# Recurrent gates from unsplit fp32 blocks, recurrence as timed events, modulation from fp32 quarter products, later sums of squares

## The chip, the cores and the metric

One core of one Trainium2 chip runs the whole program. The metric is device time in microseconds; an execution is one forward pass. The program is fixed before it starts: every engine (PE for matrix products, DVE, ACT and POOL for elementwise work, SP for issuing transfers) has its own queue, which it works off in order.

## The reference

Two layers (DEPTH = 2) over 1024 latent tokens and 256 context tokens of width 1024:

```python
m = silu(cond) @ w_mod + b_mod                  # shift, scale, gate; for c and for c_ctx
h = rmsnorm(x, norm_g) * (1 + scale) + shift
q, k, v, ga, u, gb, gm = split(h @ w_in)
# A: attention, 16 query heads, 4 key heads, q and k RMS-normalised per head of 64, rotary
# B: recurrence, for each of two directions d, on uc = centred_conv(u):
r = sigmoid(block_diag(uc, w_gates[d][0]) + b)  # 16 diagonal blocks of 64 x 64
i = sigmoid(block_diag(uc, w_gates[d][1]) + b)
log_a = -8 * r * softplus(-lam[d]); a = exp(log_a)
h_t = a_t * h_(t-1) + sqrt(1 - a_t**2) * (i * uc)_t      # direction 1 runs backwards
y = h_dir0 + h_dir1
x = x + gate * ((sigmoid(gma) * (o * silu(ga)) @ w_a + sigmoid(gmb) * (y * silu(gb)) @ w_b) @ w_out)
```

The context runs through the same weights; the last layer leaves out its context outputs.

## The kernel before

Features lie on the 128 partitions, tokens along the free axis, in three chunks: C (256 context tokens), L0 and L1 (512 latent tokens each). Every large product is a `gemm` of 8 contraction steps with three matmuls each (weights and input are both split into a rounded part and a remainder: hi·hi, hi·lo, lo·hi), in the type fp32r. `w_load` fetches a 1024 x 128 weight tile in two halves, `w_split` splits it one tile ahead: the rounded part on the engine named by `weng` ("a" is ACT, "g" is POOL), the remainder on DVE.

PE's order is written out by hand. A `Timeline` keeps an estimate of PE time (`mm` adds each matmul's cost), `tl.at(delay, fn)` puts an event on a heap, and `tl.fill(gen)` steps a generator of matmuls and runs each event that has come due. The orders of ACT, DVE, POOL and SP are made by the tile scheduler from the same program. PSUM has six buffers of the tag "s" (also "g") and two of "av". Two rings in SBUF are shared by many users: `mix` (4 buffers of 128 x 1286) and `sm` (3 of 128 x 512).

The stages in order:

- The prologue (from L606): one transfer after another brings w_mod in eight tiles of 1 MB and x in three chunks. `modulation` (L323) multiplies the two conditioning vectors by a w_mod tile in four fp32 products with a stationary operand of 2 columns; `mod_turn` copies the 2 rows out, turns them by transposes onto the partitions, and `mod_done` adds the bias. `scale_rows` makes the sums of squares of x and scales it; `modulate` makes h. `recurrent_consts` (L195) works out constants of the recurrence for each layer on DVE.
- Queries, keys and values. `Group.evac` (L464) copies a tile out and squares it; `Group.sums`, due 4.0 later, adds the squares per head with `ssq` matmuls.
- The recurrent stage (from L774), eight tiles `Lru(t)` of 128 features. Each has a gemm for u (1280 tokens) and one for the gate path g. `conv` makes uc when u is out, then splits it (`uh`, `ul`). `gate` (L820) runs twelve times a tile, for two directions, two gates and three chunks: three fp32r matmuls with a 128 x 128 block that is zero off its two diagonal 64 x 64 blocks, then a tanh on ACT out of PSUM. `coeffs` (L836) then writes the whole rest at once: exp, tanh and square on ACT, the scaled products on DVE, square roots on ACT, one product per direction on POOL, three scans on DVE, and the merge with `g2`, which goes to DRAM as `zb`. `a`, `b`, `tr` and `ti` have one buffer per direction. `evac_g` (L870) takes the tanh of g on ACT and, 0.9 later, multiplies it on DVE by g, which is read out of PSUM.
- Attention, woven with the remaining input products; it is not touched.
- The output stage. In layer 0 `modulation_side` (L346) makes sixteen blocks of 256 columns of modulation beside the products: ACT scales each w_mod piece by each conditioning value (16 operations a block), POOL adds them up (`macc`), the sum is split (`mhi` on ACT, `mlo` on DVE), and four fp32r matmuls with the selector `cond_sel` add over the partitions; `mod_turn` follows.

Of the kernel before, what the change touches and what calls it, by code (L numbers as in the profile page):

```python
# [39 lines left out]
KT = 8  # L40
# [60 lines left out]
def trunk_kernel(ctx: ExitStack, tc: tile.TileContext, xT, cc, par, wmod, win, wgate, wo,  # L101
# [45 lines left out]
    def tr(o, a):  # L147
# [5 lines left out]
    DMA.dma_start(par_sb, par)  # L153
# [4 lines left out]
    e2 = sm("e2")  # L158
    V.memset(e2[:, 0:4], 0.0)
    V.memset(e2[:, 0:4:3], 1.0)  # L160
    cond_sel = const.tile([128, 2, 2], F32R, name="condsel")
    V.tensor_copy(cond_sel, e2[:, 0:4].rearrange("p (a b) -> p a b", a=2))
# [9 lines left out]
                    pattern=[[-1, 128]], channel_multiplier=1)  # L172

# [7 lines left out]
    cs = const.tile([128, KT, 2], F32, name="cs")  # L181
    ct = const.tile([128, KT, 2], F32, name="ct")
    S.activation(ct, cc_sb, AF.Tanh, scale=0.5)
    V.scalar_tensor_tensor(cs, ct, 1.0, cc_sb, op0=OP.add, op1=OP.mult)
    V.tensor_scalar(cs, cs, 0.5, None, op0=OP.mult)
# [7 lines left out]

    def recurrent_consts(l):
        lam = p(l, "lam", 0, 16)  # L195
        t = const.tile([128, 6, 16], F32, name="spt", tag="spt")
# [124 lines left out]
    def modulation(l, i, b, half, wm, box):  # L321

        if half == 0:  # L323
            box["ps"] = ptile("s", "modps")
        ps = box["ps"]
        for k in range(4):
            mm(ps[0:2], cs[:, 4 * half + k], wm[:, k], half == 0 and k == 0, half == 1 and k == 3)
            tl.pump()
        if half == 1:
            mod_turn(l, 4 * b, 4, ps, 1.0)  # L330

    def mod_turn(l, i, n, ps, wait):

        row = sm("mrow")
        S.activation(row[0:2, 0:n * 128], ps[0:2, 0:n * 128], AF.Copy)

        def turn():
            pt = ptile("s", "modpt")
            for j in range(n):
                tl.now += 0.109  # L340
# [5 lines left out]
    def modulation_side(l, blocks, work):  # L346

        for hb in [2 * b + i for b in blocks for i in range(2)]:
            acc = work.tile([128, 2, 256], F32, name="macc", tag="macc")
            for k in range(KT):  # L350
                if k % 4 == 0:
                    wm = mix("wm")[:, 0:1024].rearrange("p (k n) -> p k n", k=4)
                    DMA.dma_start(wm, wmod[l, k * 128:(k + 4) * 128, hb * 256:(hb + 1) * 256]
                                  .rearrange("(k p) n -> p k n", p=128))
                w = wm[:, k % 4]
                t = acc if k == 0 else sm("wmt").rearrange("p (s n) -> p s n", s=2)
# [4 lines left out]
                yield  # L361

            for _ in range(4):
                yield
            hi = sm("mhi", F32R).rearrange("p (s n) -> p s n", s=2)
            lo = sm("mlo", F32R).rearrange("p (s n) -> p s n", s=2)
            S.activation(hi, acc, AF.Copy)
            V.tensor_sub(lo, acc, r32(hi))
            for _ in range(3):
                yield  # L370
            ps = ptile("av", "modps")
            for x, part in enumerate((hi, lo)):
                for s in range(2):
                    mm(ps[0:2, 0:256], cond_sel[:, s], part[:, s], x + s == 0, x + s == 2)
            mod_turn(l, 2 * hb, 2, ps, 3.0)
# [76 lines left out]
    class Group:  # L452
# [10 lines left out]
        def evac(self, i, c, ps):  # L463
# [9 lines left out]
            if c == part[-1]:  # L473
                tl.at(4.0, lambda: self.sums(i, part, o))
# [134 lines left out]
    with tc.tile_pool(name="prep", bufs=1, reuse_waits="tile") as work:  # L609
        xs, arrive = {}, {}  # L610
# [15 lines left out]
        def scale_rows(c):  # L626
# [18 lines left out]
            def bcast():  # L645
# [4 lines left out]
                for k in range(KT):  # L650
                    if c == "L1":
# [10 lines left out]
        def modulate(c, k0, nk=4):  # L662

            n = CH[c][1]
# [676 lines left out]
```

## Time and profile before

| | us |
|---|---|
| median of 3 runs | 3177.37 (lowest 3171.86) |
| profiled execution, its own time | 3176.29 |
| profiled execution, span from first to last instruction | 3174.5 |
| PE busy in it | 3049.5 |

A row of the profile names an engine, a line of the kernel and `output<-inputs` by the program's names (L145 is the helper that issues all matmuls, so the output's name tells them apart). The length of a matmul's row goes on beyond the start of the next; what one costs in a row of many is the distance between starts.

### The profile page before, as it was taken

The page shows a single profiled execution, that of the slowest core. Times are in us where ns is not written, and L with a number is a line of the kernel's source. Part 1 is how long each engine was busy: PE and PEld are TensorE (multiplying, and loading weights), DVE is VectorE, ACT ScalarE, POOL GpSimd, SP SyncE. Part 2 cuts the span into 40 slices and gives each one's busy share as a digit, 9 for nine tenths or more (in the row PEclk, how much of TensorE's full clock was granted, in tenths as well). Part 3 has the DMA queues.
Part 4 walks back from the last instruction along what each step waited for, and adds up shares of the span by engine and source line. Part 5 has one row for each costly group of instructions (what it writes and reads, how often), then busy time and mean ns, then how long its engine had stood idle before and what let it go on. Part 6 is the DMA issues. An engine that isn't in the chain of part 4 may idle for free.

```text
span 3174.5 us, 42428 instructions
## 1 busy us (share of the span) xinstructions
PE 3049.5 (96%) x14592; PEld 2459.1 (77%) x14592; DVE 2453.9 (77%) x3675; ACT 1715.0 (54%) x3060; POOL 1024.5 (32%) x777
## 2 busy tenths in 40 slices
PE   7999999999999999999999999999999999999999
PEld 3788778788777777887777778777777777777887
DVE  7665887589989998556685776897799989996544
ACT  4323767466666666445654324676476666663222
POOL 0211444134334434245522222333244444441000
PEclk9999999999999999999999999999999999999999
DMA  5443111421222222254555452111412121115554
GB/s 197 145 149 126 44 57 50 125 63 54 76 68 82 60 62 75 97 189 158 170 196 175 135 176 71 58 47 53 123 55 76 58 75 58 55 58 173 183 173 140
DMA packets 243416, 332.08 MB, mean 105 GB/s; under 512 B 63664, under 2 KB 109552, under 8 KB 242944
## 3 DMA queue, kind: packets, MB, share of 16 engines
q1 hardware_dynamic: 243200, 329.37, 32.6%
q8 instruction: 115, 1.88, 0.2%
q14 instruction: 101, 0.83, 0.1%
HBM read 252.54 MB, written 76.58 MB: 104 GB/s over the span
## 4 chain that ended last, share of the span: by engine, by line
PE 53%; DVE 19%; issue 6%; ACT 4%; DMA 4%; POOL 3%; SPq 0%; DVEq 0%; POOLq 0%; ACTq 0%
PE gps L145 29%; PE avps L145 8%; PE s2ps L145 7%; PE s1ps L145 4%; DVE pl L1008 3%; DVE wlo L227 3%; DVE mp L979 2%; PE lps L145 2%; POOL macc L360 2%; PE gtps L145 1%; DVE ti L856 1%; PE qps L145 1%; POOL b L853 1%; DVE g L867 1%; PE vps L145 1%
## 5 line engine op out<-in xcount | busy, mean ns | idle before, releaser
L145 PE MATMUL gps<-h,whi 128*128 128x512 f32 x3328 | 1042.3, 394 | 18.3 <-DVE g L876 15.9
L145 PEld LDWEIGHTS gps<-h,whi 128*128 128x128 f32 x3328 | 613.5, 190 | 135.3 <-issue 10.7
L1008 DVE TENSOR_TENSOR pl<-pf,ph 128x512 fp32r<-128x512 f32 x656 | 627.2, 957 | 71.3 <-ACT ph L1007 67.9
L145 PE MATMUL gps<-h,wlo 128*128 128x512 f32 x1664 | 655.2, 394 | 1.4 <-DVE wlo L227 1.4
L1006 ACT ACTIVATE pf<-s2ps 128x512 f32<-128x512 f32 x656 | 392.9, 599 | 343.1 <-PE s2ps L145 171.7
L1022 POOL TENSOR_TENSOR acc<-pf 128x512 f32<-128x512 f32 x256 | 353.0, 1379 | 686.4 <-ACT pf L1006 686.2
L979 DVE TENSOR_REDUCE mp<-s1ps 128x1 f32<-128x512 f32 (+1 forms) x800 | 453.7, 584 | 59.9 <-PE s1ps L145 56.5
L1007 ACT ACTIVATE ph<-s2ps 128x512 fp32r<-128x512 f32 x656 | 390.0, 595 | 0.0
L227 DVE TENSOR_TENSOR wlo<-wraw,whi 128x512 fp32r<-128x512 f32 x392 | 330.8, 865 | 62.2 <-ACT whi L226 33.0
L226 ACT ACTIVATE whi<-wraw 128x512 fp32r<-128x512 f32 x324 | 194.6, 628 | 340.9 <-PE gps L145 269.1
L145 PEld LDWEIGHTS gps<-h,wlo 128*128 128x128 f32 x1664 | 314.3, 189 | 71.4 <-DVE wlo L227 2.2
L145 PE MATMUL s1ps<-k,qa 128*128 128x512 f32 (+1 forms) x800 | 287.3, 368 | 15.9 <-DMA qa<-q0L 10.7
L145 PEld LDWEIGHTS s1ps<-k,qa 128*128 128x128 f32 x800 | 244.5, 310 | 55.4 <-DVE mp L979 10.6
L145 PE MATMUL avps<-pl,vv 128*128 128x512 f32 x656 | 262.4, 400 | 8.0 <-DVE pl L1008 7.7
L145 PE MATMUL avps<-ph,vv 128*128 128x512 f32 x656 | 266.2, 406 | 0.0
L145 PE MATMUL s2ps<-qa,k 128*128 128x512 f32 x656 | 260.8, 398 | 4.4 <-DVE mp L979 3.4
L145 PE MATMUL s2ps<-qb,k 65*128 65x512 f32 x656 | 262.5, 400 | 0.1
L145 PE MATMUL gps<-e,whi 128*128 128x512 f32 x768 | 244.8, 399 | 0.4 <-DVE e L227 0.2
L360 POOL TENSOR_TENSOR macc<-macc,wmt 128x512 f32<-128x512 f32 x112 | 156.6, 1398 | 252.3 <-ACT wmt L358 228.0
L1024 POOL TENSOR_TENSOR acc<-acc,pf 128x512 f32<-128x512 f32 x128 | 183.1, 1430 | 79.4 <-ACT pf L1006 77.4
L145 PE MATMUL qps<-h,whi 128*128 128x512 f32 x640 | 203.6, 399 | 1.7 <-DVE h L674 0.9
L145 PE MATMUL gps<-c,whi 128*128 128x256 f32 x1024 | 197.8, 289 | 2.7 <-DVE c L222 1.9
(214 smaller groups left out, 4945.0 us busy)
## 6 DMA issues: line engine op xcount, KB each, us to landing
wraw<-in_win_dram SPq DMA_DIRECT2D x200, 256.0 KB
wraw<-in_wo_dram SPq DMA_DIRECT2D x192, 256.0 KB
wm<-in_wmod_dram SPq DMA_DIRECT2D x32, 512.0 KB
wm<-in_wmod_dram SPq DMA_DIRECT2D x8, 1024.0 KB
rb<-rq SPq DMA_DIRECT2D x64, 128.0 KB
k<-k SPq DMA_DIRECT2D x24, 320.0 KB
v<-vst SPq DMA_DIRECT2D x20, 256.0 KB
vv<-v SPq DMA_DIRECT2D x8, 640.0 KB
```

What stands on the lines that cost most here:

```text
L145: nc.tensor.matmul(o, a, b, start=start, stop=stop)
L226: S.activation(dst_hi, src, AF.Copy)
L227: (V if lo_eng == "v" else G).tensor_sub(dst_lo, src, r32(dst_hi))
L360: G.tensor_add(acc, acc, t)
L853: G.tensor_mul(a2, a2, ti)
L856: V.tensor_tensor_scan(h, a, a2, 0.0, op0=OP.mult, op1=OP.add)
L979: tl.at(0.3, lambda: V.reduce_max(self.mp[:, j, b:b + 1], ps[:, :n], axis=AX.X))
L1006: S.activation(pf, ps, AF.Exp)
L1007: S.activation(ph, ps, AF.Exp)
L1008: tl.at(1.4, lambda: V.tensor_sub(pl, pf, r32(ph)))
L1022: G.tensor_add(self.acc_tile(x), first, pf)
L1024: G.tensor_add(self.accs[x], self.accs[x], pf)
```

## The change

Six edits:

1. The gates. The 64 x 64 blocks are loaded alone (`gw`) and multiplied unsplit, in fp32: per chunk eight products of 64 rows by 64 columns, in two groups of four (one per gate), each of the four on another pair of row half and column half. Direction 1 lands with its two halves of 64 features exchanged; so its constants are loaded exchanged (`recurrent_params`), uc is copied to an exchanged `us`, and its scan's output is exchanged back into `a1`, all by transfers. `gate` runs three times a tile, 3.6 apart, with four PSUM buffers at a time. The split of uc and of the blocks goes.
2. `coeffs` becomes thirteen events over 26 units of PE time. `ti` gets a second buffer; `c0` gets a buffer of its own in place of one of `mix`.
3. `evac_g` copies g out of PSUM on ACT as well; the DVE multiplication reads SBUF and is due at 2.5.
4. In the recurrent stage weights are split with ACT, as elsewhere (`weng` is no longer switched).
5. The modulation, in the prologue and beside the output stage: the stationary operand is padded to 32 columns, four products go to four quarters of the output partitions, and a matmul with `sel4` adds the quarters while it turns them.
6. `Group.sums` is due at 7.0 in place of 4.0. `recurrent_consts` waits for its later loaded parameters.

```diff
+    def recurrent_params():
+        DMA.dma_start(par_sb[:, :, lam_c:lam_c + 8], par[:, :, lam_c:lam_c + 8])
+        for a, n in ((gate_c + 16, 16), (lam_c + 8, 8)):
+            for h in range(2):
+                DMA.dma_start(par_sb[64 * h:64 * h + 64, :, a:a + n], par[64 - 64 * h:128 - 64 * h, :, a:a + n])
...
+    def mod_half(ps, half, wm, n):
+        for k in range(4):
+            mm(ps[32 * k:32 * k + 32, :n], csp[:, 4 * half + k], wm[:, k], half == 0, half == 1, 0.215 * n / 512)
...
-                nc.tensor.transpose(pt[:, 2 * j:2 * j + 2], row[0:2, j * 128:(j + 1) * 128], ident[0:2, 0:2])
+                mm(pt[:, 2 * j:2 * j + 2], row[:, j * 128:(j + 1) * 128], sel4, True, True, 0.2)
...
-                for s in range(2):
-                    S.activation(t[:, s], w, AF.Copy, scale=cs[:, k, s:s + 1])
-                if k:
-                    G.tensor_add(acc, acc, t)
...
+            for half in range(2):
+                mod_half(ps, half, wms[half], 256)
...
-                tl.at(4.0, lambda: self.sums(i, part, o))
+                tl.at(7.0, lambda: self.sums(i, part, o))
...
-        weng[0] = "g"
...
-                    self.uh, self.ul = self.wt("uh", dt=F32R), self.wt("ul", dt=F32R)
-                    split(self.uh, self.ul, uc)
...
-                    tl.at(28.0 if last else 36.0, self.gate)
+                    self.us = self.exchange(uc, self.wt("us"))
+                    self.tg = [[self.wt(f"tr{d}"), self.wt(f"ti{d}", 2)] for d in range(2)]
+                    self.todo = ["C", "L0", "L1"]
+                    tl.at(20.0 if last else 24.0, self.gate)
+                def exchange(self, a, b):
+                    DMA.dma_start(b[0:64], a[64:128])
+                    DMA.dma_start(b[64:128], a[0:64])
+                    return b
...
-                    mm(ps[:, :n], gh[:, dg], uh[:, off:off + n], True, False)
-                    mm(ps[:, :n], gh[:, dg], ul[:, off:off + n], False, False)
-                    mm(ps[:, :n], gl[:, dg], uh[:, off:off + n], False, True)
...
+                    ps = [ptile("s", "gtps") for _ in range(4)]
+                    for gi in range(2):
+                        for h in range(2):
+                            rows = slice(64 * h, 64 * h + 64)
+                            for d in range(2):
+                                o = 64 * (h ^ d)
+                                mm(ps[2 * gi + d][o:o + 64, :n], self.gw[rows, 2 * d + gi], self.uc[rows, off:off + n],
+                                   True, True, 0.03 + 0.245 * n / 512)
...
+                    for at, fn, *d in ((0, decay, 1), (0.5, gated, 1), (2, gated, 0), (4.5, decay, 0), (5, square, 1),
+                                       (9.5, square, 0), (11, root), (14, product, 1), (17, product, 0),
+                                       (17.5, scan, 1), (21.5, scan, 0), (22, self.exchange, i1, a1), (26, merge)):
+                        tl.at(at, lambda fn=fn, d=d: fn(*d))
...
+                    S.activation(g, ps[:, :n], AF.Copy)
+                    tl.at(2.5, lambda: V.scalar_tensor_tensor(g, th[:, :n], 1.0, g, op0=OP.add, op1=OP.mult))
```

## Rows read from the trace of the kernel before

**Rows 1.** The page's first part: busy time of each engine, share, instructions.

```profile
PE 3049.5 (96%) x14592; PEld 2459.1 (77%) x14592; DVE 2453.9 (77%) x3675; ACT 1715.0 (54%) x3060; POOL 1024.5 (32%) x777
```

**Rows 2.** Windows by stage: length, PE, PEld, DVE, ACT, POOL busy, clock, DMA.

```profile
250.00:575.00 325.00, 309.98 (x1578) 263.01 (x1578) 237.79 (x205) 213.13 (x259) 123.28 (x98) 0.99 0.20 65
...
1314.00:1745.00 431.00, 408.96 (x2063) 338.76 (x2062) 271.15 (x438) 220.74 (x470) 156.96 (x113) 0.97 0.54 176
...
1909.00:2225.00 316.00, 293.87 (x1382) 243.90 (x1381) 254.38 (x181) 194.03 (x236) 108.97 (x93) 0.97 0.16 54
```

**Rows 3.** PE's waits, recurrent stage of layer 0: us, times, longest.

```profile
PE gps L145 <- DVE g L876: 8.5, 7, 2.2
PE gtps L145 <- ACT ti L829: 4.8, 3, 3.0
```

**Rows 4.** The same for layer 1.

```profile
PE gtps L145 <- DVE g L876: 11.7, 3, 5.2
PE gps L145 <- DVE g L876: 7.4, 4, 2.9
```

**Rows 5.** PE's timeline, gates in the recurrent stage: start, us, instructions.

```profile
300.28 0.28 PE L145 MATMUL gtps<-uh,gh 128*128 128x256 f32 x1
...
300.64 0.63 PE L145 MATMUL gps<-h,whi 128*128 128x512 f32 x2
...
301.34 0.40 PE L145 MATMUL gtps<-uh,gh 128*128 128x512 f32 x1
...
302.04 0.40 PE L145 MATMUL gtps<-uh,gh 128*128 128x512 f32 x1
```

**Rows 6.** PE's timeline in attention: four fp32 products to four quarters.

```profile
651.92 1.06 PE L145 MATMUL lps<-acc,ones 128*32 128x512 f32 x8
652.91 0.50 PE L145 MATMUL avps<-ph,vv 128*128 128x512 f32 x1
```

**Rows 7.** Windows of one recurrent tile, layer 0.

```profile
441.50:478.20 36.70, 35.16 (x181) 29.81 (x180) 30.93 (x25) 26.23 (x32) 17.40 (x13) 1.00 0.16 54
```

**Rows 8.** Groups of instructions: ACT's weight split and a copy out of PSUM.

```profile
L226 ACT ACTIVATE whi<-wraw 128x512 fp32r<-128x512 f32 x324 | 194.6, 628 | 340.9 <-PE gps L145 269.1 <-issue 36.4 <-PE qps L145 21.8
...
L797 ACT ACTIVATE up<-gps 128x512 f32<-128x512 f32 (+1 forms) x48 | 24.2, 525 | 88.4 <-PE gps L145 88.4
```

**Rows 9.** Recurrence of one tile, ACT's and DVE's timelines: first exponential, last merge.

```profile
412.47 1.45 ACT L844 ACTIVATE a<-tr,sp 128x1280 f32<-128x1280 f32 x1
...
444.49 2.78 DVE L867 SCALAR_TENSOR_TENSOR g<-ti,g 128x512 f32<-128x512 f32 x2 [1.18 <-POOL ti L866]
```

**Rows 10.** Windows of the prologue and its end.

```profile
18.50:51.80 33.30, 27.91 (x82) 8.61 (x81) 24.08 (x59) 16.64 (x33) 0.00 (x0) 0.85 0.76 274
51.80:77.00 25.20, 21.07 (x125) 16.83 (x124) 22.88 (x52) 15.94 (x28) 0.00 (x0) 1.00 0.07 22
```

**Rows 11.** PE's timeline in the prologue.

```profile
24.11 1.05 PE L145 MATMUL ssn<-ones,sqa 128*128 128x1 f32 x8 [1.14 <-DVE sqa L395]
...
31.37 0.41 PE L341 MATMUL modpt<-ident,mrow 2*128 2x2 f32 x4
...
47.41 4.45 PE L145 MATMUL modps<-wm,cs 128*2 128x512 f32 x10
```

**Rows 12.** PE's waits, 52 to 262 us, then 1750 to 1919 us.

```profile
PE ssq L145 <- ACT sqq L472: 6.4, 3, 3.0
...
PE ssq L145 <- ACT sqq L472: 8.6, 3, 6.5
```

**Rows 13.** PE's waits, output stage of layer 0.

```profile
PE modps L145 <- ACT mhi L367: 7.4, 4, 4.3
...
PE modps L145 <- DVE mlo L368: 3.8, 6, 1.6
```

**Rows 14.** The chain of waits, 585 to 960 us: two of its transfers.

```profile
592.19 6.61 DMA qa<-q0L
...
897.79 2.30 DMA l2L<-rq
```

More of the change, by code (lines that the diff above doesn't have):

```diff
@@ L319, in mod_done, with modulation @@
             V.tensor_scalar(gt, m[:, 16:24], 0.5, None, op0=OP.mult)
-    def modulation(l, i, b, half, wm, box):
+    def mod_half(ps, half, wm, n):
+        for k in range(4):
+            mm(ps[32 * k:32 * k + 32, :n], csp[:, 4 * half + k], wm[:, k], half == 0, half == 1, 0.215 * n / 512)
+    def modulation(l, b, half, wm, box):
         if half == 0:
             box["ps"] = ptile("s", "modps")
[L325 to L328, printed above, removed]
+        mod_half(box["ps"], half, wm, 512)
+        tl.pump()
         if half == 1:
-            mod_turn(l, 4 * b, 4, ps, 1.0)
+            mod_turn(l, 4 * b, 4, box["ps"], 1.0)
     def mod_turn(l, i, n, ps, wait):
         row = sm("mrow")
-        S.activation(row[0:2, 0:n * 128], ps[0:2, 0:n * 128], AF.Copy)
+        S.activation(row[:, 0:n * 128], ps[:, 0:n * 128], AF.Copy)
         def turn():
@@ L363, in modulation_side @@
+            wms = []
+            for half in range(2):
+                wm = mix("wm")[:, 0:1024].rearrange("p (k n) -> p k n", k=4)
+                DMA.dma_start(wm, wmod[l, half * 512:half * 512 + 512, hb * 256:(hb + 1) * 256]
+                              .rearrange("(k p) n -> p k n", p=128))
+                wms.append(wm)
+                for _ in range(3):
+                    yield
             for _ in range(4):
                 yield
-            hi = sm("mhi", F32R).rearrange("p (s n) -> p s n", s=2)
@@ L366, in modulation_side @@
[L366 to L369, printed above, removed]
-                yield
[L371 to L375, printed above, removed]
+            ps = ptile("av", "modps")
@@ L378, in trunk_kernel @@
+            for half in range(2):
+                mod_half(ps, half, wms[half], 256)
+            mod_turn(l, 2 * hb, 2, ps, 3.0)
+            for _ in range(4):
+                yield
     HS = {"L0": ("h0", "h1"), "L1": ("h2", "h3"), "C": ("c0", "c1")}
@@ L650, in bcast @@
                 for k in range(KT):
+                    scaled.add(c)
                     if c == "L1":
@@ L662, in modulate @@
         def modulate(c, k0, nk=4):
+            assert c in scaled
             n = CH[c][1]
@@ L847, in coeffs @@
[L847 to L854 removed]
+                        S.activation(b, a, AF.Square)
@@ new lines, in gated, with square, root @@
+                    def gated(d):
+                        i = co[d][2]
+                        V.scalar_tensor_tensor(i, i, 1.0, self.us if d else self.uc, op0=OP.add, op1=OP.mult)
+                    def square(d):
+                        b = co[d][1]
+                        V.scalar_tensor_tensor(b, b, 1.0, self.tg[d][0], op0=OP.add, op1=OP.mult)
+                    def root():
+                        for d in range(2):
+                            S.activation(co[d][1], co[d][1], AF.Sqrt, scale=0.25)
@@ L1258, in trunk_kernel @@
                 mod_start(l + 1)
-                side = modulation_side(l, (4, 5), work) if l == 0 else iter(())
-                tl.fill(weave(ga, itertools.chain(side, modulation_side(l + 1, (0, 2, 1, 3), work)), 0.5))
-            tl.fill(halves(1, nxt) if last else weave(halves(1, nxt), modulation_side(l + 1, (4, 5), work), 0.36))
+                side = modulation_side(l, (4, 5)) if l == 0 else iter(())
+                tl.fill(weave(ga, itertools.chain(side, modulation_side(l + 1, (0, 2, 1, 3))), 0.5))
+            tl.fill(halves(1, nxt) if last else weave(halves(1, nxt), modulation_side(l + 1, (4, 5)), 0.36))
             x_src = x_new
```

117 lines of the change are left out of this document (48 added, 69 removed).

## The prediction

> **What bounds the kernel now.** I read the page's busy times first: PE 3049.5 of 3174.5 us, the next engine DVE at 77% [rows 1]. So a change can win in two ways only: by giving PE less to do, or by removing a stretch in which PE stands still, and what DVE, ACT or POOL save elsewhere is worth nothing by itself. Then I cut the span into stages [rows 2] and asked of each for PE's waits. The two recurrent stages stand out: PE is busy 309.98 of 325 us in layer 0 and 293.87 of 316 in layer 1, 37 us of standing still, and here DVE (254.38 of 316 in layer 1) and ACT are heavily used too. What ends the waits is mostly one line: L876, the DVE multiplication that reads the g product out of PSUM [rows 3, 4]; until it is done PE has no free PSUM buffer. The granted clock is a little below full in these stages too (0.99 and 0.97). Two smaller places of the same kind are the sums of squares [rows 12] and the modulation beside the output stage [rows 13]. All sums are made against the profiled execution, 3176.3 us with 1.8 us outside its span; the median of the runs shown is 1.1 us above it, which I leave out.
>
> **The gates' products.** Today a gate and direction costs three matmuls per chunk. From start to start that is 300.64 − 300.28 = 0.36 us for 256 tokens and 302.04 − 301.34 = 0.70 us for 512 [rows 5]; a set of three chunks is 1.76, four sets 7.04 a tile, and sixteen tiles 113 us of PE. The new products are fp32, in groups of four on separate quarters of the array. No row shows 64-row quarters. The nearest row has four fp32 products of 512 columns that go to four quarters of the output: eight records, and the next matmul starts 652.91 − 651.92 = 0.99 us later [rows 6]. One such product alone takes two records of 0.445 us (ten in 4.45 us [rows 11]), 0.89 us, so the four of the row run side by side. I take 0.99 for a 512 chunk and, by half the columns and the same start, 0.55 for 256: a tile is 2 × (0.99 + 0.99 + 0.55) = 5.06 us, sixteen are 81 us. The term is **−32 us**. The bounds: the same four one after another, 3.6 us a group, make it +210; side by side without any start (0.89 and 0.45) −41. I take the row because the change addresses quarters in the same way, with two of its four split by input rows in place of output columns.
>
> **The waits in the recurrent stages.** Copying g out on ACT releases its PSUM buffer without DVE, so L876's waits (8.5 + 11.7 + 7.4 = 27.6 us [rows 3, 4]) go. What is late next is ACT. In a tile of layer 0 it is busy 26.23 of 36.70 us [rows 7]; it gains four weight splits of 0.628 and three copies of about 0.525 [rows 8], 4.1 us, while the tile gets shorter: PE's 35.16 less 1.98 is 33.2. So ACT comes to about 30.3 of 33.7 us, and it alone now frees the PSUM of the gates, which take four of six buffers at a time. Today's waits for ACT's gate tanh are 4.8 us in layer 0 [rows 3]; I add half a microsecond a tile, 8 us, between 0 and all of the 27.6 given back. DVE is relieved: the splits of uc and of the blocks leave it. POOL's 17.4 us a tile fall as the weight split leaves it. Net **−20 us**. With fewer stops I count a third of the clock's loss in these stages back (0.03 × 316 + 0.01 × 325 = 12.7): **−4**, between 0 and −13.
>
> The second buffer of `ti`, the own buffer of `c0` and the thirteen events I cost at nothing: they change when things are asked for, and PE's gemms (over 27 us of each tile) cover them, as long as a tile's recurrence ends within a tile's period; that is the third rival. The four exchange transfers a tile stand in SP's queue, with weight loads behind them; a wait there is harmless while the next tile's weights, asked for 3.5 units into a gemm of about 13 us, come in time. Landings on the chain go from 2.30 to 6.61 us [rows 14], the range for an exchange. `recurrent_params` (five small transfers) and the constants leave the prologue and are needed some 200 us later: nothing.
>
> **The prologue.** Each w_mod tile costs eight records of 0.445 us, 3.56 us, and then 0.99: PE gives up 20 us over eight tiles. But DVE is what remains: 24.08 and 22.88 us of work between 18.5 and 77 us [rows 10], when x's first chunk is in. Without a pause that ends at 65.5, so 11.5 us is the most to gain and nothing the least. The scaling chain (squares, sum, root, scale) has pauses of its own: **−8**.
>
> **Sums of squares.** PE waits 6.4 and 8.6 us for ACT's squares [rows 12], at six places, the longest 6.5. Due three units later, waits up to 3 us vanish and longer ones shrink by 3: the 6.4 of the first three go, of the other three 2.1 go and the long one keeps 3.5. That is 11.5; no PE work is added. I take **−12**, between −15 and 0, since ACT's queue may itself be what is late.
>
> **The modulation beside the output stage.** The waits for `mhi` and `mlo`, 7.4 + 3.8 = 11.2 us [rows 13], go with the two operations. PE gets more: per block two groups of four at 0.55 for four matmuls at 0.12 (0.36 / 3 [rows 5]), and two fp32 turns at 0.26 (1.05 us for eight records, four products [rows 11]) for two transposes at 0.10 (0.41 / 4 [rows 11]): 1.62 − 0.68 = 0.94, by sixteen blocks +15. Net **+4**; with ACT and POOL freed of the scaling, other waits of the stage (22 us of PE standing still [rows 2]) may go too, so −10 to +15.
>
> **Sum.** −32 − 20 − 4 − 8 − 12 + 4 = −72: 3176.3 − 72 = **3104 us**.
>
> A rule of the Trainium skill speaks against the first term. The four products of a lps group [rows 6] differ in output quarter alone; the new ones also differ in input rows, and two on different row halves write the two halves of one PSUM buffer. "TensorEngine Tiling (Array Packing)", section "Restrictions and Gotchas", says that different row tiles cannot access the same PSUM bank simultaneously, and no run here shows such a pair yet. By that rule, only two of each four go together; the first rival is the price of it.
>
> **The rivals.**
>
> *Pairs.* Only two of four products run together. Each pair then takes what the four take in rows 6, so a tile's gates take 10.1 us and sixteen 162, 81 more than I count: 3185 us, no gain at all. For it: no row shows products on different input rows side by side. Against: column quarters do run side by side at full rate. One by one would be 3104 + 3 × 81 = 3347.
>
> *ACT takes DVE's place.* ACT at 30.3 of 33.7 us queues the gates' tanh behind exponentials of about 1.45 us, and PE waits for it as long as it waited for L876: +20, and the clock's 4 stay lost, 3128 us. For it: today's 4.8 us for ACT at a lower load. Against: six PSUM buffers give slack.
>
> *The recurrence sets the period* (this one ends slower). `a`, `b` and `tr` have one buffer per direction. Today a tile's recurrence runs from its first exponential at 412.47 to the last merge at 444.49 + 2.78 = 447.27, 34.8 us of a period of 36.7 [rows 9, 7]. The change adds an exchange before the merge, and `a1` is its target, so the next tile's first exponential of direction 1 waits for the merge. If the 34.8 stay and 4.5 are added (the middle of rows 14), the period is 39.3: against 36.7 in layer 0 and 33.8 in layer 1 (one chunk of g less, 24 × 0.12) that is 8 × 2.6 + 8 × 5.5 = +65 in place of −56: 3225 us. It decides from the point where exponential to merge exceeds the 33.7 us that PE leaves. For it: the 34.8. Against: direction 1 goes first, its first exponential is no longer written before the other direction's gates, and `ti` is doubled; by its events the stretch is 26 units.
>
> **How the numbers follow.** The forecast has 0.60, with the terms' bounds some 40 us either way; ACT in DVE's place 0.17; pairs 0.08; the recurrence 0.11; one by one 0.04. Faster by over 2% (about what a measurement of this kernel can tell) means under 3113.8 us: four fifths of the forecast and a fifth of the ACT case, 0.51. Slower by over 2% means above 3240.9: one by one and a little of the recurrence, 0.06. The rest, 0.43, is within 2%. The range of 8 in 10 is 3060 to 3185, which holds the pairs; the forecast's own is 3065 to 3145.
>
> **What would show it.** Right: the gates' eight records of a 512 chunk and gate end about 1 us after they begin; no wait of PE for L876's successor; a tile period near 33.7 us in layer 0; qps starting near 44 us in place of 51.8; no wait for `mhi`. Wrong: gates at 2 us a group (pairs); waits of PE for tanh or weight splits of over 2 us a tile (ACT); `decay` waiting for the merge of the tile before, or transfers of weights that come late behind an exchange (the recurrence). If the recurrent stages together lose less than 30 us, the forecast is wrong in its main term.

## The result, and the profile after

The changed kernel takes 3090.47 us (median of 4 runs, 3085.53 to 3092.98) against 3174.86 for the kernel before beside it: a ratio of 0.974, 95% interval 0.972 to 0.976. One of the four runs of before took 9001.91 us; it counts in the medians, 3174.86 here and 3177.37 in the section on the time before, but not in the ratio. The forecast was 3104. The profiled execution took 3085.53 us, 90.8 less than that of before, and its span is 3083.8 us. All sums below are made within these two executions. That of the kernel after is the fastest of its four; by the ratio the gain is 83 us.

The page's first part of the kernel after, to be held against [rows 1]:

```profile
PE 2995.5 (97%) x15024; PEld 2380.3 (77%) x15024; DVE 2315.7 (75%) x3610; ACT 1651.4 (54%) x2898; POOL 788.4 (26%) x581
```

PE is busy 54.0 us less than before and the span is 90.7 shorter; so some 37 us of the gain is time in which PE stood still. The other engines' savings (DVE 138, ACT 64, POOL 236 us) are, as said, worth nothing by themselves. Where the time went, by the starts of PE's first products of each kind in the two timelines (for the end of attention, of its last one):

| stretch | before, us | after, us | change | forecast |
|---|---|---|---|---|
| to the first query product | 51.8 | 49.9 | -1.9 | -8 |
| queries, keys, values, layer 0 | 194.4 | 191.1 | -3.3 | sums of squares |
| recurrent stage, layer 0 | 352.8 | 326.8 | -26.0 | together -56 |
| attention, layer 0 | 715.0 | 713.1 | -1.8 | 0 |
| output stage, layer 0 | 422.6 | 408.1 | -14.5 | +4 |
| queries, keys, values, layer 1 | 168.2 | 157.7 | -10.5 | sums, both layers: -12 |
| recurrent stage, layer 1 | 333.3 | 300.4 | -32.9 | (above) |
| the rest, to the end of the span | 936.6 | 936.7 | +0.1 | 0 |

A difference of 3 us in the second or third row says nothing by itself: in the runs further down that leave these stretches as they are, the second takes 191.0 to 194.8 us and the third 323.6 to 325.9.

The windows by stage of the kernel after (the two recurrent stages, the output stage, and the middle of the first recurrent stage), which answer to [rows 2]:

```profile
257.50:558.00 300.50, 291.65 (x1655) 222.35 (x1654) 218.18 (x181) 228.06 (x306) 89.86 (x60) 0.98 0.36 101
1862.00:2135.00 273.00, 265.78 (x1434) 197.23 (x1433) 201.38 (x159) 220.63 (x287) 75.36 (x50) 0.99 0.35 100
1290.00:1690.00 400.00, 394.55 (x2209) 325.98 (x2208) 209.03 (x405) 101.12 (x188) 0.00 (x0) 0.99 0.56 182
365.00:510.00 145.00, 145.00 (x822) 110.43 (x821) 111.28 (x89) 123.12 (x164) 49.88 (x31) 1.00 0.32 91
```

In the middle of the recurrent stage PE is busy 145.00 of 145 us. ACT has become the next engine, 123 of 145, as expected; but no wait for it is left in layer 0 but one of 0.2 us. PE's waits of the two recurrent stages, for [rows 3, 4]:

```profile
PE gps L145 <- DVE wlo L233: 8.6, 2, 8.3
PE gtps L145 <- ACT tr L836: 0.2, 1, 0.2
...
PE gtps L145 <- ACT tr L836: 5.8, 1, 5.8
PE gps L145 <- DVE wlo L233: 1.5, 1, 1.5
```

The 32.4 us of [rows 3, 4], 37.1 with the smaller waits of these stages, have become 16.1, and nearly all of them are three waits late in the stages. PE's timeline, gates of one tile (start, length, instructions, two records each product), for [rows 5]:

```profile
377.02 1.09 PE L145 MATMUL gtps<-uc,gw 64*64 64x256 f32 x16
378.05 0.51 PE L145 MATMUL gps<-c,whi 128*128 128x256 f32 x2
...
380.71 1.95 PE L145 MATMUL gtps<-uc,gw 64*64 64x512 f32 x16
382.59 0.73 PE L145 MATMUL gps<-h,whi 128*128 128x512 f32 x2
```

From start to start the eight products of a 512 chunk take 1.88 us and those of the 256 chunk 1.03: a tile's gates take 2 x 1.88 + 1.03 = 4.78 us in place of 7.04. ACT's first exponential of every second tile in layer 0:

```profile
357.95 1.46 ACT L853 ACTIVATE a<-tr,sp 128x1280 f32<-128x1280 f32 x1
...
424.96 1.46 ACT L853 ACTIVATE a<-tr,sp 128x1280 f32<-128x1280 f32 x1
...
491.86 1.46 ACT L853 ACTIVATE a<-tr,sp 128x1280 f32<-128x1280 f32 x1
```

Two tiles are 67.0 us apart, 33.5 a tile; 33.7 had been worked out.

### The profile page after: what moved, and what is told of

It reads as the page before. It is cut to its first block, busy times and chain, and to the rows that moved or that the text cites. A ratio compares the mean times of both kernels' runs of the same rounds, so it can differ in the third digit from the quotient of the medians.

```text
span 3083.8 us, 42886 instructions
## 1 busy us (share of the span) xinstructions
PE 2995.5 (97%) x15024; PEld 2380.3 (77%) x15024; DVE 2315.7 (75%) x3610; ACT 1651.4 (54%) x2898; POOL 788.4 (26%) x581
## 5 line engine op out<-in xcount | busy, mean ns | idle before, releaser
L232 ACT ACTIVATE whi<-wraw 128x512 fp32r<-128x512 f32 x392 | 235.4, 630 | 438.8 <-PE gps L145 327.4
L233 DVE TENSOR_TENSOR wlo<-wraw,whi 128x512 fp32r<-128x512 f32 x392 | 271.8, 713 | 57.7 <-ACT whi L232 51.2
L145 PE MATMUL s1ps<-k,qa 128*128 128x512 f32 (+1 forms) x800 | 287.0, 368 | 13.5 <-DMA qa<-q0L 7.7
L526 POOL TENSOR_TENSOR t<-qg,rc 128x512 f32<-128x512 f32 x40 | 60.8, 1521 | 703.0 <-DMA rc<-in_ropec_dram 511.9
```

The lines of the kernel that those rows point to most:

```text
L145: nc.tensor.matmul(o, a, b, start=start, stop=stop)
L232: S.activation(dst_hi, src, AF.Copy)
L233: (V if lo_eng == "v" else G).tensor_sub(dst_lo, src, r32(dst_hi))
L526: G.tensor_mul(t1, a, rc[:, o:o + n])
```

## The experiments

Four runs undo or alter one part each, four ask why the parts gave what they gave, and four follow what these showed. Ratios are to the kernel before, run beside each on the same chip. Its median was 3175 us beside the first four and 3178 beside the others, and its three runs in the ratio of the kernel after took 3171.86, 3172.35 and 3177.37. So medians alone don't show a difference of 6 us or less between versions that were timed apart.

**The old gates.** The recurrent gates, the splits of uc and of the blocks and the recurrence written at once come back, with one buffer of `ti`, `c0` in `mix` and no exchange; the copy of g and the weights' split on ACT stay.

```diff
-                                mm(ps[2 * gi + d][o:o + 64, :n], self.gw[rows, 2 * d + gi], self.uc[rows, off:off + n],
...
+                    mm(ps[:, :n], gh[:, dg], uh[:, off:off + n], True, False)
+                    mm(ps[:, :n], gh[:, dg], ul[:, off:off + n], False, False)
+                    mm(ps[:, :n], gl[:, dg], uh[:, off:off + n], False, True)
```

> The changed kernel with the recurrent gates, the split of uc and the recurrence written at once as in the kernel before; the copy of g on ACT, the weight split on ACT, the modulation and the later sums stay. PE theory (gates are worth their PE time): sixteen tiles cost 7.04 in place of 4.78 us, so about 36 us more than the changed kernel, near 3126 us, and the windows of a recurrent tile are longer by 2.3 us with PE as busy as before. Rival (PE is not the bound of this stage, the waits were): near 3095 us. Rival (the timed events and the DVE work saved matter as much as the matmuls): 3150 us or more, with new waits of PE for ACT or DVE.

3164.4 us, ratio 0.996 (0.995 to 0.998): 74 us more than the kernel after, twice what PE's shorter gates make ((7.04 - 4.78) x 16 = 36). PE's waits in its recurrent stages, layer 0 and then layer 1:

```profile
PE gps L145 <- DVE wlo L230: 17.2, 5, 5.8
PE gtps L145 <- ACT tr L824: 4.4, 1, 4.4
...
PE gps L145 <- DVE wlo L230: 14.2, 7, 3.1
...
PE gtps L145 <- ACT tr L824: 5.7, 1, 5.7
```

With the smaller ones they come to some 47 us against 16.1 in the kernel after, 31 more. With the 36 us of the products that is 67 of the 71 us by which the two stages (365.5 and 332.3 us) are longer. So the rival holds: what the change took from DVE and POOL in the recurrent stage, and the order and the buffers of what is left, count about as much as the shorter products. Which of these it is, this run doesn't tell.

**g read out of PSUM by DVE, as before.**

```diff
-                    S.activation(g, ps[:, :n], AF.Copy)
-                    tl.at(2.5, lambda: V.scalar_tensor_tensor(g, th[:, :n], 1.0, g, op0=OP.add, op1=OP.mult))
+                    tl.at(0.9, lambda: V.scalar_tensor_tensor(g, th[:, :n], 1.0, ps[:, :n], op0=OP.add, op1=OP.mult))
```

> The changed kernel, only that DVE again reads g out of PSUM for its multiplication, 0.9 after the tanh, and ACT does not copy it. Theory (the PSUM buffer held for DVE was the wait): 20 to 28 us more than the changed kernel, 3110 to 3118 us, with PE waiting for that DVE line as in rows 3 and 4. Rival (DVE is relieved of the splits and so comes in time by itself): 3088 to 3096 us, no such wait above 5 us in all.

3131.4 us, ratio 0.986 (0.984 to 0.987): 41 us more than after. PE's waits for that multiplication, layer 0 and layer 1:

```profile
PE gtps L145 <- DVE g L903: 13.6, 4, 3.4
...
PE gtps L145 <- DVE g L903: 19.6, 4, 5.0
```

33.2 us, more than the 27.6 of before. That the gates now ask for four PSUM buffers at once would explain the more; it wasn't separated. The rest fits the clock: granted 0.94 in the stretch 1990 to 2110 us of layer 1, where the kernel after has 0.97.

**The old modulation beside the output stage.**

```diff
-                mod_half(ps, half, wms[half], 256)
...
+                for s in range(2):
+                    S.activation(t[:, s], w, AF.Copy, scale=csp[:, k, s:s + 1])
+                if k:
+                    G.tensor_add(acc, acc, t)
...
+            S.activation(hi, acc, AF.Copy)
+            V.tensor_sub(lo, acc, r32(hi))
```

> The changed kernel with the modulation beside layer 0's output stage as before (scaling on ACT, sums on POOL, four fp32r selector matmuls, transposes). Theory (its waits cost more than the quarter products add to PE): some 14 us more, 3105 us, with waits for mhi and mlo of about 11 us. Rival (the stage gained from other edits, and the quarter products cost as much PE time as they save): 3085 to 3094 us.

3106.2 us, ratio 0.978 (0.976 to 0.979): 16 more than after, all of it in the output stage (427.1 us against 408.1). Its waits and the window of the stage:

```profile
PE modps L145 <- ACT mhi L383: 10.0, 6, 5.0
PE modps L145 <- DVE mlo L384: 4.6, 6, 1.7
```

```profile
1290.00:1708.00 418.00, 393.45 (x1977) 326.61 (x1976) 263.28 (x417) 214.13 (x457) 156.53 (x112) 0.96 0.55 175
```

PE is busy as long in these 418 us as after in 400 (393.45 and 394.55). What differs are the waits, and the clock: 0.96 here, 0.99 after.

**Sums of squares due at 4.0 again.**

```diff
-                tl.at(7.0, lambda: self.sums(i, part, o))
+                tl.at(4.0, lambda: self.sums(i, part, o))
```

> The changed kernel with the sums of squares due at 4.0 again. Theory (the delay removes PE's waits for the squares): 12 to 15 us more, near 3103 us, with waits of ssq for ACT's squares of about 15 us in both layers. Rival (the waits went because of other edits, among them the constants that moved): 3088 to 3096 us.

3097.8 us, ratio 0.976 (0.974 to 0.977): 7 us more than after, less than the theory's. The row for the queries of layer 1:

```profile
PE ssq L145 <- ACT sqq L468: 8.4, 3, 5.2
```

With 2.4 in layer 0 it is 10.8 us, against 1.4 and 2.3 left in the kernel after (the 2.3 are for a later step of ACT, not for the squares). The difference of 7.1 is that of the medians, but the intervals of the two ratios overlap and the two profiled executions lie 16 us apart, so the size is open. The theory took the 15.0 of [rows 12]; here, with the other edits in place, they are 10.8.

**One quarter of the array at a time.** The order of a chunk's eight products: by quarter, the two gates of one innermost (the 16 of the text below are records, two a product; each quarter has two products).

```diff
-                    for gi in range(2):
-                        for h in range(2):
-                            rows = slice(64 * h, 64 * h + 64)
-                            for d in range(2):
+                    for h in range(2):
+                        rows = slice(64 * h, 64 * h + 64)
+                        for d in range(2):
+                            for gi in range(2):
```

> The 16 gate products of a recurrent tile and gate are issued quarter by quarter: the four input blocks of one quarter of the array stand back to back, then those of the next quarter; products, data and tile sizes are those of the kernel after. Theory (products in different quarters run at the same time because neighbours in the order lie in different quarters): the quarters then run nearly one after another, the 512-column chunk of a gate takes between 3 and 7.5 us for its 16 products in place of 1.88 us, TensorE's gate work of a tile goes from 4.8 to 8.5 us or more, and 16 tiles cost about 60 us or more: about 3150 us, ratio to the kernel before 0.99. Rival (TensorE looks far enough ahead for the order not to matter, the quarters overlap anyway): chunk near 1.9 us, 3087 to 3095 us.

3102.6 us, ratio 0.976 (0.975 to 0.978). PE's timeline, one chunk of 512:

```profile
387.87 1.97 PE L145 MATMUL gtps<-uc,gw 64*64 64x512 f32 x16
389.77 0.73 PE L145 MATMUL gps<-h,whi 128*128 128x512 f32 x2
```

1.90 us in place of 1.88: the theory falls, the quarters run side by side whether neighbours in the order lie in different ones or not. The whole is still 12 us slower (11 against the run with the exchange on POOL's queue, further down, on the same chip). Eight of these lie in the gates, which come to 95.2 us with their pauses in place of 87.3: about every second tile has a chunk of 2.3 to 4.3 us, where the kernel after has three such chunks in all. That this order asks for all four PSUM buffers at once, where the kernel after can begin with two, would explain it; it wasn't separated.

**The weights' split on POOL in the recurrent stage.**

```diff
+        weng[0] = "g"
```

> In the recurrent stage alone the high parts and remainders of the next layer's weights go to GpSimd in place of ScalarE and VectorE; the rest is the kernel after. Theory (the recurrent stage is bound by TensorE, which is busy 145.0 of 145 us in its middle, so what the other engines carry matters only where a weight comes late at the end of a stage): within 8 us of the kernel after, 3085 to 3100 us. Rival 1 (ScalarE, 123 of 145 us busy, sets the pace beside TensorE): faster, 3070 to 3083 us. Rival 2 (GpSimd's split comes later than the products want it): waits of the products for a high part or remainder, 3105 us or more.

3103.6 us, ratio 0.977 (0.975 to 0.978). The middle of the first recurrent stage:

```profile
365.00:510.00 145.00, 142.06 (x806) 107.57 (x805) 122.75 (x92) 106.50 (x138) 67.39 (x46) 0.99 0.32 90
```

The edit moves only the high parts, and those of the next tile; the remainders stay on DVE, unlike what the expectation says. ACT falls from 123.12 to 106.50 us and PE loses 2.94. ACT didn't set the pace; it has room for the split. On POOL a half of a weight tile takes 1.05 us (median) where ACT takes 0.63, and PE's waits for high parts and remainders in layer 0 are 13.8 us in place of 8.6. The time lies just beyond the theory's range, at the edge of rival 2.

**The last w_mod tile ahead of C's sums, in the prologue.** In the kernel after PE stands there as its timeline shows:

```profile
46.23 0.98 PE L145 MATMUL ssn<-ones,sqa 128*128 128x1 f32 x4 [9.73 <-DVE sqa L391]
47.15 1.93 PE L145 MATMUL modps<-wm,csp 128*32 128x512 f32 x8
...
49.88 1.20 PE L145 MATMUL qps<-h,whi 128*128 128x512 f32 x2
```

```diff
-                tl.at(5.0 if c != "C" else 3.5, sums2)
+                tl.at(5.0 if c != "C" else 8.0, sums2)
...
-        tl.at(1.0, lambda: modulate("C", 0))
+        tl.at(3.2, lambda: modulate("C", 0))
...
-        tl.at(4.0, lambda: modulate("C", 4))
+        tl.at(5.0, lambda: modulate("C", 4))
```

> In the prologue the sums of squares of C come later and its modulation with them, so that the products of the last w_mod tile go ahead of C's sums on TensorE; the rest is the kernel after. Theory (of the 8 us that the prologue was to gain only 2.0 us came, because TensorE stood 9.7 us for C's squares with the modulation's last tile queued behind them): the first query product starts at about 43 to 47 us in place of 49.6 us and the time falls by 3 to 8 us to about 3084 us. Rival (VectorE's own work sets the prologue: the products for the query wait for the modulated layer L0 as before, in whatever order TensorE stands): no change, 3088 to 3093 us.

3089.3 us, ratio 0.972 (0.970 to 0.974). The first query product starts at 38.8 us in place of 49.9, and the values of layer 0 begin at 214.5 in place of 211.5, where runs that leave the prologue alone have 211.5 to 215.6: the eleven microseconds won are all given back. The windows of 40 to 70 us of this run:

```profile
40.00:50.00 10.00, 3.49 (x13) 2.92 (x13) 6.76 (x19) 3.98 (x9) 0.00 (x0) 0.58 0.39 119
50.00:60.00 10.00, 7.84 (x32) 6.45 (x32) 10.00 (x29) 8.59 (x16) 0.00 (x0) 0.74 0.15 52
60.00:70.00 10.00, 5.53 (x31) 4.55 (x31) 8.07 (x19) 4.10 (x8) 0.00 (x0) 0.94 0.00 1
```

DVE is busy all of 50 to 60 us: the rival's place. The time is the rival's too, no change.

**The exchange transfers on POOL's queue.** In the kernel after, SP's queue at the end of layer 0's recurrent stage:

```profile
525.68 0.32 SPq L917 DMA_DIRECT2D gm8L<-gmt  x1
542.29 0.47 SPq L817 DMA_DIRECT2D a<-ti  x1
...
545.47 0.34 SPq L267 DMA_DIRECT2D wraw<-in_win_dram  x1
```

It stands 16.2 us behind an exchange that waits for its scan, with a weight load behind it.

```diff
-                    DMA.dma_start(b[0:64], a[64:128])
-                    DMA.dma_start(b[64:128], a[0:64])
+                    G.dma_start(b[0:64], a[64:128])
+                    G.dma_start(b[64:128], a[0:64])
```

> The exchange transfers of the recurrent stage (copying states across partitions) are issued from GpSimd's queue in place of SyncE's; the rest is the kernel after. Theory (at the end of each recurrent stage SyncE's queue stands about 17 us behind the last exchange, which waits for its scan, so that the last weight load comes late and TensorE waits 8.3 us for a remainder in layer 0, and 5.8 us and about 7.9 us in layer 1): those waits go, 5 to 15 us faster, 3075 to 3086 us. Rival 1 (the late remainder comes from the engines that split it, not from the load): no change, 3087 to 3093 us. Rival 2 (GpSimd's own work is now queued behind the waiting exchanges): slower, 3097 us or more, with new waits for what GpSimd makes.

3091.8 us, ratio 0.972 (0.971 to 0.974), no change, and PE's wait in layer 0 is still 8.3 us; in layer 1 the waits are 7.8 and 6.9 us in place of 5.8 and 7.7. The queue's pause was a bystander: rival 1. With the exchange gone from the queue, the weight load still is issued only at 543.59 us (545.47 in the kernel after), when DVE's split has freed its buffer.

**The split ahead of the last scans.** DVE's timeline in the kernel after shows what the remainder was queued behind:

```profile
536.39 3.36 DVE L877 TENSOR_TENSOR_SCAN ti<-a,b 128x256 f32<-128x256 f32 x1 [4.20 <-POOL b L870]
...
542.06 2.80 DVE L875 TENSOR_TENSOR_SCAN ti<-a,b 128x1280 f32<-128x1280 f32 x1
544.78 1.87 DVE L233 TENSOR_TENSOR wlo<-wraw,whi 128x512 fp32r<-128x512 f32 x3
```

DVE idles 4.20 us before the scans, and the remainder that PE waits for comes after them; on ACT its high part (534.32 us) stands in the same way behind the square roots.

```diff
                 def coeffs(self):
-
+                    if self.t == 7: tl.at(10.0, lambda: w_split(pos[0] + 1))
```

> One event more in the last recurrent tile of a layer: the split of the next weight block stands ahead of the tile's square roots and scans, where the kernel after has it behind them; the rest is the kernel after. Theory (TensorE's 8.3 us wait for a remainder at the end of layer 0's recurrent stage comes from VectorE, which stands in order: the remainder is queued behind three scans that wait for GpSimd's products, and not from the load): the 8.3 us wait goes, layer 1's 1.5 us too, and the time falls by 6 to 9 us, to about 3083 us. Rival 1 (the load of the block is late): the wait stays, 3087 to 3093 us. Rival 2 (the scans, now 1.3 us later, hold back the merge and the attention stage instead): the wait goes and a new one of the same size comes, no change in time.

3086.4 us, ratio 0.971 (0.970 to 0.972). DVE's timeline, and what PE waits for at that place now:

```profile
534.08 1.28 DVE L233 TENSOR_TENSOR wlo<-wraw,whi 128x512 fp32r<-128x512 f32 x2
539.39 3.44 DVE L877 TENSOR_TENSOR_SCAN ti<-a,b 128x256 f32<-128x256 f32 x1 [4.03 <-POOL b L870]
```

```profile
PE s1ps L145 <- DMA qa<-q0L: 6.7, 1, 6.7
```

The 8.3 us wait is gone, and the stage takes 320.7 us, where the kernel after has 326.8 and the runs that leave it alone 323.6 and more. But the first scores of attention now wait 6.7 us for their queries, and the median is 4 us lower, not 6 to 9: theory for the wait's cause, and in part rival 2 for its worth. The queries' first transfer is issued at 558.15 in place of 554.74 us, behind the stores of the later merge: that is 3.4 of the 6.7 us. The kernel before waits 5.7 us at this place, and the kernel after, held up by 8.3 us ahead of it, not at all. In layer 1 the wait of 1.5 us doesn't go (1.4), against the theory, and the first scores wait 9.5 us in place of 7.7.

**The sums on POOL, in the prologue.**

```diff
-            V.tensor_add(sqa[c][:, :n], sqa[c][:, :n], sq[:, :n])
+            (eng or V).tensor_add(sqa[c][:, :n], sqa[c][:, :n], sq[:, :n])
...
-                    sq_add(work, c, j, xs[c][:, j])
+                    sq_add(work, c, j, xs[c][:, j], V if c == "L0" else G)
```

> The order of the run with the last w_mod tile ahead of C's sums, and besides the additions of the squares of C and L1 in the prologue go from VectorE to GpSimd, which does nothing there; the rest is the kernel after. Theory (VectorE's work is what the prologue cannot get under: it is busy all of 50 to 60 us and 8.1 of the 10 us after that in that run; 14 additions, 3.4 and 5.3 us, leave it): TensorE's waits of 6.6 us for the sums and some of those for the modulated C shrink, 4 to 10 us faster than the kernel after, about 3084 us. Rival 1 (GpSimd's additions, at 0.9 us for 256 elements and 1.4 for 512, are slower and the sums come no earlier): 3087 to 3097 us. Rival 2 (the data's arrival sets the prologue): first query product early, its later ones wait as before, 3088 to 3093 us.

3090.7 us, ratio 0.972 (0.971 to 0.974): no change. PE's waits up to 90 us:

```profile
PE qps L145 <- ACT whi L232: 6.1, 1, 6.1
PE qps L145 <- DVE c L672: 5.7, 4, 2.1
```

The waits for the squares are gone; the weights' high part and the modulated C came in their place, and the values of layer 0 begin at 214.4. Three orders of the prologue with the first query product at 49.9, 38.8 and 43.1 us all bring the values at 211 to 215. PE's waits up to 90 us come to 31.0, 32.7 and 33.4 us in them: they change their places only. That taking 14 additions off DVE doesn't move it speaks against DVE's load as the only limit; what is, stays open.

**The recurrence at once, one buffer for the input gates, with the new gates.**

```diff
-                    self.tg = [[self.wt(f"tr{d}"), self.wt(f"ti{d}", 2)] for d in range(2)]
+                    self.tg = [[self.wt(f"tr{d}"), self.wt(f"ti{d}")] for d in range(2)]
...
-                        tl.at(at, lambda fn=fn, d=d: fn(*d))
+                    for fn, *d in ((decay, 0), (square, 0), (gated, 0), (decay, 1), (square, 1), (gated, 1), (root,),
+                                   (product, 0), (scan, 0), (product, 1), (scan, 1), (self.exchange, i1, a1), (merge,)):
+                        fn(*d)
```

> The new gates and all else of the kernel after, but the recurrence of a tile is written at once, with no events, forward direction first, and its input gates have one buffer each. It splits the 74 us by which the kernel after beats the one with the old gates, of which TensorE's shorter gates make (7.04 - 4.78) x 16 = 36 us. Theory (the remaining 38 us come from the events: written at once, the scans stand in VectorE's queue ahead of the weight remainders that TensorE needs, as the waits of 17.2 and 14.2 us for a remainder in that run show): 20 to 40 us slower than the kernel after, 3110 to 3130 us, with such waits. Rival (they come from VectorE's splitting of the gate input and of the gate weights, which this run doesn't have): 3088 to 3098 us.

3249.4 us, ratio 1.023 (1.021 to 1.024): 159 us more than after, far off both expectations, and slower than the kernel before. ACT's waits in layer 0, and PE's:

```profile
ACT ti L836 <- DMA a<-ti: 33.8, 4, 9.3
ACT ti L836 <- DVE g L888: 15.4, 4, 3.9
```

```profile
PE gps L145 <- DVE wlo L233: 39.0, 4, 11.1
PE gtps L145 <- ACT ti L836: 22.7, 4, 5.8
```

```profile
257.00:632.00 375.00, 313.26 (x1669) 234.84 (x1668) 208.92 (x183) 221.22 (x302) 89.77 (x60) 0.91 0.29 81
```

With one buffer, the tanh of a tile's input gate waits up to 9.3 us until the exchange and the merge of the tile before have read it; it holds the gates' PSUM, and what stands behind it on ACT, the weights' high parts among it, is late by as much. From the first gemm to the first scores of attention the two stages are 71 and 86 us longer than in the kernel after. Some 117 us of this are PE standing still; the other 41 us are PE busy for longer with the same products, at a granted clock of 0.92 and 0.89 over the stages, where the kernel after has 0.98. So the 159 are accounted for. The run takes away the events and the buffers and puts the forward direction first, and doesn't part these; the ACT rows belong to the buffers, PE's 39.0 to all.

**Both small edits together** (the split ahead of the last scans, and the prologue with the sums on POOL).

> The edit of the run with the split ahead of the last scans and those of the run with the sums on GpSimd together. Theory (the two lie in different stages and add): 3090 less the gains of both, 3074 to 3082 us by what is expected of each. Rival (one of them gives nothing): the gain of the other alone.

3083.8 us (3082.8 to 3087.5), ratio 0.971 (0.969 to 0.972), the best of all versions, against 0.974 (0.972 to 0.976) of the kernel after. Its first query product starts at 43.3 us, its values at 214.7: the rival, the gain is that of the first edit alone, 0.3% of the time of before. The two intervals only just part. On one chip the run with the sums on POOL alone took 3088.5 to 3093.6 us, and this one, which adds the earlier split, 3082.8 to 3087.5.

## Why the prediction was right, and where it was not

The forecast of 3104 was 13.5 us above the median; the kind of result (faster by over 2%) and the main mechanism came as worked out. By its terms:

- **The gates' products, -32: right, 36 measured.** 0.94 us a group of four at 512 columns, 0.99 taken from [rows 6]; 0.51 at 256, 0.55 taken. The pairs rival is out: products on different input rows whose results fall into two halves of one PSUM buffer go at full rate, four in 0.94 us where one alone takes 0.89 [rows 11]. The Trainium skill, "TensorEngine Tiling (Array Packing)", section "Restrictions and Gotchas", says that different row tiles cannot access the same PSUM bank simultaneously; the 0.94 us do not agree with that where the two write different halves of the partitions. The price of the rival one by one was worked out wrong: four of 0.89 us (0.45 for 256 tokens) come to 17.8 us a tile, +172 us in place of +210, and the time to about 3308 in place of 3347.
- **The recurrent waits, -20: right in size, 37.1 to 16.1 us, wrong in what is left.** I expected half a microsecond of waiting for ACT in each tile. ACT is loaded nearly as I said (123.12 of 145 us, which is 28.4 us in a tile of 33.5, where I had 30.3), and in mid-stage of layer 0 PE doesn't wait for it. What is left are single waits late in the stages. The 8.3 us are DVE's remainder behind the scans of the last recurrence, whose remaining events run all at once at the end of the stage, ahead of the next weights; the run with the earlier split shows it. The 5.8 us in layer 1 are put down to ACT's tanh, but ACT itself stood 6.30 us (to 2101.49) for a weight load, whose split stands ahead of that tanh; the load was issued at 2098.56, as soon as DVE's split, behind the scans of the tile before, had freed a buffer. So the late engine is DVE, by its order, and not ACT by its load. No run moves that split alone. The g copy, undone, costs 41 us, so this term is worth more with the new gates than the 27.6 us of the old rows.
- **The clock, -4: about right.** The granted clock in the recurrent stages goes from 0.99 to 0.98 and from 0.97 to 0.99, some 3 us.
- **The prologue, -8: wrong, 1.9 measured.** The step that failed was "DVE is what remains". PE's order is fixed: a wait of 9.73 us for C's squares held the last modulation tile behind it, and the modulated h with it. And that limit wasn't the only one, as the orders that lift it gain nothing. The transfers of w_mod, which the prediction left out, are another: PE's waits up to 90 us rise from 19.3 to 31.0 us, and this is the largest of them, where the kernel before has 0.3:

```profile
PE modps L145 <- DMA wm<-in_wmod_dram: 14.2, 5, 7.5
```

  Which of the limits comes last stays open.
- **The sums of squares, -12: right.** Waits of 15.0 us [rows 12] became 3.7; undoing the edit gives back 7 us by the medians. That the other edits help there too would explain the rest; it isn't shown.
- **The modulation beside the output stage, +4: wrong in sign, -14.5 measured, and 16 by undoing it.** The PE work added was overrated: a block takes 1.00 + 0.36 us in place of the 1.62 that I had counted, by rows of the kernel after:

```profile
1412.98 1.07 PE L145 MATMUL modps<-wm,csp 128*32 128x256 f32 x16
1413.98 0.50 PE L145 MATMUL gps<-c,whi 128*128 128x256 f32 x2
...
1417.89 0.50 PE L145 MATMUL modpt<-sel,mrow 128*128 128x2 f32 x4
1418.25 0.72 PE L145 MATMUL gps<-h,whi 128*128 128x512 f32 x2
```

  That is 11 us of PE added ((1.36 - 0.68) x 16). Against it stand all of the 11.2 us of waits [rows 13] and some more for what ACT and DVE owed beside the scaling (PE stands still 5 us of the stage in place of 22), and the clock, which I left out of this term: 0.97 before [rows 2], 0.99 after, 2% of 400 us.
- **The second buffer of `ti` and the events, at nothing: wrong.** They are not free cover for a change that works without them; the run without both is 159 us slower. The third rival, the recurrence that sets the period, was a true mechanism, though by another buffer than I named: not `a1`, whose exponential waits for the merge, but `ti`, whose tanh waits for the exchange. These parts of the change, together, are what keeps it from happening; what each does alone isn't shown. I had named `ti`'s doubling among the reasons against that rival, but put no price on it.

The terms as measured, -36 - 21 - 3 - 2 - 11 - 14.5, come to some -88 of the 90.8 us between the two profiled executions. By the ratio, with 83 us in all, they are together a few microseconds too large. The two wrong terms err in opposite ways, the prologue 6 us short and the modulation 18 us better, so a part of the total's nearness is luck.

## What to carry to other kernels

Price an edit in the company of the others: a recurrence written at once is 11 us faster than the kernel before with the long gates (3164) and 71 us slower with the short ones and their exchange (3249), and a copy out of PSUM was worth 28 us by the old rows and 41 by the new. Where a queue of an in-order engine looks idle before a wait, look for what is queued behind the waiting instruction; the pause that is easiest to see (SP's 16 us) may be a bystander, and a run that takes it away alone says so. A wait put down to one engine may belong to what that engine stood for: the 5.8 us for ACT's tanh were a weight load ahead of it. A stage that ends by flushing its remaining events deserves a look of its own: there the next stage's first inputs should go ahead.

## What the runs showed that was not expected

- Eight fp32 products of 64 rows by 64 columns and 512 tokens took 1.88 us in the order that alternates the quarters and 1.90 us in the one that doesn't.
- DVE's scan of 256 elements takes 0.69 us, or 3.4 us, longer than the scan of 1280 (2.80 us):

```profile
441.74 3.42 DVE L877 TENSOR_TENSOR_SCAN ti<-a,b 128x256 f32<-128x256 f32 x1 [4.52 <-POOL b L870]
...
473.34 0.69 DVE L877 TENSOR_TENSOR_SCAN ti<-a,b 128x256 f32<-128x256 f32 x1 [2.84 <-POOL b L870]
```

  In the kernel after it is 3.4 us in ten tiles of sixteen, and in each of these POOL is busy with the other direction's product for 2.8 to 2.9 us of it; in the six of 0.69 us POOL stands still. In the kernel before all sixteen take 0.66 to 0.69 us, with POOL standing still. That is some 27 us of DVE's time, and 2.7 of them lie in the scans ahead of the remainder that PE waits 8.3 us for. What the two engines share isn't shown.
- A pause of PE in the prologue left its clock lower. The windows of 50 to 60 us, of the kernel after and of the kernel before:

```profile
50.00:60.00 10.00, 8.92 (x26) 6.86 (x25) 9.73 (x27) 9.26 (x17) 0.00 (x0) 0.50 0.16 52
```

```profile
50.00:60.00 10.00, 8.27 (x31) 4.52 (x30) 9.97 (x24) 8.43 (x16) 0.00 (x0) 1.00 0.17 53
```

  After the pause of 9.73 us that ended at 46.23 the granted clock is 0.50, the lower of its two levels (1.2 GHz), where before, with PE busy 8.22 of the 10 us ahead, it is 1.00. Query products of 512 columns stand 0.43 us apart there (50.88 to 51.31 us) against 0.23 later (282.60 to 282.83), so a part of what the prologue won was paid back in the first query products.
